# A hybrid retention and attention block: mean squares from a second, token-major load of x, a reordered opening, and re-dealt helper work

## The chip, the cores and the metric

The kernel runs on one core of a Trainium2 chip. The metric is the device time of one execution in microseconds (us); the median of three runs is compared. A core has five engines with instruction streams of their own: TensorE (matmuls), VectorE, ScalarE, GpSimd and SyncE. In the profile they are PE, DVE, ACT, POOL and SP. Each works through its stream in order and waits where an instruction needs something from another engine or from a DMA.

## The reference

One encoder layer over 1024 tokens with 16 learned meta tokens in front (T = 1040), D = 1024, all in float32. Cut to what matters:

```python
def _rms_norm(x, w):
    y = xf * lax.rsqrt(jnp.mean(xf * xf, axis=-1, keepdims=True) + EPS)
    return (y * w).astype(x.dtype)

u = RMSNorm(h)                 # h: meta tokens, then x
z = u @ w_in                   # one combined projection: q, k, v, gates of both branches
A: bidirectional retention     # 4 heads of 128 (v: 256), 8 chunks of 128 and the meta chunk,
                               # decays exp(rel * log_gamma), forward and backward scans,
                               # k * k_decay summed into states, group norm, SiLU gate, projection
B: windowed attention (+-128)  # 8 heads, 2 key groups, rotary, meta keys always seen, sink logit,
                               # SiLU gate, projection
out = x + RMSNorm((sigmoid(gA) * yA + sigmoid(gB) * yB) @ w_out)
```

The mean of squares of each token is thus needed by everything behind the first normalisation. The kernel projects x times the norm's weight, without the division, and brings the division in later, per token, as a factor.

## The kernel before

**Products.** A float32 product is made of three matmuls of rounded parts: high by high, low by high and high by low (`mm3`, L75 to L81). Each matrix is split for it: the high part is a rounding copy (ScalarE or GpSimd), the low part is the original less the high part (VectorE: `dve_lo`, L94, for weights, L335 for x). x comes feature-major: eight k-tiles `xr0` to `xr7` of 128 features by 1040 tokens. Their high and low parts are `xh`, `xl` (tiles named `big`).

**The opening** (L262 to L396, pool "setup"). For each k-tile, ScalarE makes the high part (L333) and VectorE the low part (L335), and `qk0_mm(k)` issues 18 matmuls: q and k of retention head 0, in six accumulator banks (`pq`, `pk`), each `mm3` over one piece of the tokens. ScalarE squares each `xr` tile (L354), and VectorE adds the eight squares up (`add_square`, L327). The sum is split (`sqh`, `sql`), and 18 small matmuls with a tile of ones (`sums_by_rows`, L376) bring the sums into a bank `pms`, one row per token. From it VectorE makes `ms` (mean squares plus EPS, L385, L386), `r2` and `kdr` (the factors of k in the states). The decays of the heads come out of `dec` by a logarithm's series (L210 to L239: `exponentials`, `decays`, `decay_series`, `decay_exponents`) in tiny VectorE instructions, and become tables (`decay_table`: its argument `dd` on VectorE, L247, its exponential `DT` on ScalarE, L249).

**Evacuation and the first values.** `evac_qk0(i)` takes one of the six q and k banks through the rotary formula: three VectorE multiplications (L190 to L192) and an addition on GpSimd. `projT` gives the values of one token block: block 0 is the meta tokens (`pv0_0`, matmuls L165 and L167, from `xm`, which `pack_meta` packs at L157), blocks 1, 2 and so on use `mm3`. The accumulators of the tag "pj" have three banks. So `pv0_1` waits for evacuation 0 to free one, `pv0_2` for another, `pv0_3` for `pv0_0`'s and `pv0_4` for `pv0_1`'s, which `vh_1` (ScalarE, L494) and `vl_1` (VectorE, L94) read.

**Loads.** SyncE issues the loads in the order of the text, and ScalarE's queue carries the first half of `xr0` and two small ones, `dect` and `idx` (L288, L289). `load_w` loads two raw halves of a weight unit and splits them.

**What sets the order.** The framework puts the instructions of each engine in an order by simulating their times, and an instruction under `issue_after` (or `follow`) comes behind the one named there. In attention, a chunk's work is written with `fill` ahead of and behind its scores: `fill(n)` takes n units of matmul work from a list of generators (query projections, gate products), after the table `FILL`. Helper works, such as loading, scaling and splitting for later parts, start at the yields which the table `BEGUN` names: `half_w` (half of a weight's split), `sum_fetch`, `sum_scale` and `sum_row` (x tiles `xs` for sums by rows), `load_k`, `pre_low` (low part of early gate weights).

Of the kernel before, what the change touches and what calls it, by code (L numbers as in the profile page):

```python
# [7 lines left out]
F32 = mybir.dt.float32  # L8
R = mybir.dt.float32r
# [18 lines left out]
FILL = (((5, 6),) * 1 + ((5, 5),) * 1 + ((4, 4),) * 1 + ((4, 3),) * 1 + ((4, 5),) * 2 + ((4, 7),) * 1 + ((4,  # L28
        5),) * 1 + ((6, 4),) * 1 + ((4, 4),) * 1 + ((4, 3),) * 1 + ((4, 4),) * 1 + ((4, 5),) * 2 + ((1, 4),)
        * 1 + ((6, 3),) * 1 + ((4, 5),) * 2 + ((4, 4),) * 1 + ((5, 4),) * 1 + ((3, 4),) * 1 + ((4, 3),) * 1 +  # L30
        ((4, 4),) * 4 + ((5, 4),) * 1 + ((3, 4),) * 1 + ((4, 4),) * 1)
# [12 lines left out]
def block_kernel(ctx: ExitStack, tc: tile.TileContext, xT, x, w_in, w_rb, w_ab, w_out, vecs, dec, sink,  # L44
# [156 lines left out]
    ones, onef = (ra.tile([P, 2], t, name=n) for n, t in (("ones", R), ("onef", F32)))  # L201
# [24 lines left out]
    def decay_series():  # L226
        v = nc.vector
        for j in (15, 13, 11, 9, 7, 5, 3):
            v.scalar_tensor_tensor(acc, acc, 1.0 / j, ss, op0=ALU.add, op1=ALU.mult)
        v.scalar_tensor_tensor(acc, acc, 1.0, s_, op0=ALU.add, op1=ALU.mult)  # L230
        v.scalar_tensor_tensor(lg, acc, -2.0, lg, op0=ALU.mult, op1=ALU.add)
# [35 lines left out]
    with tc.tile_pool(name="setup", bufs=1, reuse_waits="tile") as st:  # L267
# [19 lines left out]
        with tc.issue_after(nc.scalar.activation(warm, warm, AF.Exp).ins):  # L287
            nc.scalar.dma_start(dect, dec.partition_broadcast(P))  # L288
            nc.scalar.dma_start(idx, tab[:, MW + 3 * P:])  # L289
# [6 lines left out]
        nc.sync.dma_start(xr[2], xT[2])  # L296
        nc.sync.dma_start(xr[3], xT[3])
# [3 lines left out]
        nc.sync.dma_start(cr, rope[0])  # L301
        nc.sync.dma_start(sr, rope[1])
        nc.sync.dma_start(tabt[:, 0:3 * P], tab[:, MW:MW + 3 * P])
# [17 lines left out]
        nc.vector.memset(onef, 1.0)  # L321
        nc.vector.tensor_copy(ones, onef)
        nc.vector.memset(ms, 1.0)
        low, squares, sums = None, [], {}

        def add_square(k):
            sums[k] = nc.vector.tensor_tensor(squares[k], squares[k - 1], squares[k], ALU.add).ins  # L327

        for k in range(KT):
            t = xr[k]  # L330
            parts = [(0, 528), (528, T)] if k == 0 else [(0, T)]
            for a, b in parts:
                nc.scalar.activation(xh[k][:, a:b], t[:, a:b], AF.Copy, scale=vec[:, k:k + 1])  # L333
                with tc.issue_after(sums[k - 2] if k > 3 else exponents) if k > 2 else ExitStack():
                    low = nc.vector.scalar_tensor_tensor(xl[k][:, a:b], t[:, a:b], vec[:, k:k + 1],  # L335
                                                         xh[k][:, a:b].bitcast(F32), op0=ALU.mult, op1=ALU.subtract)
            if k == 2:
                with tc.issue_after(low.ins):
                    decays()
                    decay_series()  # L340
                    exponents = decay_exponents()
                decay_columns()
            if k == 0:
                with tc.issue_after(low.ins), tc.issue_after(raised[1]):
                    exponentials()
                    nc.gpsimd.tensor_tensor(e, ecst[:, 0:8], na, ALU.pow)
            if k == 1:
                third()
            if k == 3:
                with tc.issue_after(exponents):  # L350
                    fifth()
            qk0_mm(k)
            squares.append(st.tile([P, T], F32, tag="sq", bufs=4, name=f"sq{k}"))
            nc.scalar.activation(squares[k], t, AF.Square)  # L354
# [3 lines left out]
        with tc.issue_after(low.ins):  # L358
            pack_meta()
            wv0 = load_w(w_in, U_V, act=True)  # L360

        add_square(KT - 1)
        with tc.issue_after(sums[KT - 1]):
            rotated = evac_qk0(0)
        sq = squares[-1]
        sqh, sql = (st.tile([P, T], R, name=n) for n in ("sqh", "sql"))
        nc.scalar.copy(sqh, sq)
        with tc.issue_after(rotated):
            split = dve_lo(sql, sq, sqh)
        pms = p1("pms")  # L370

        def sums_by_rows(k):
            for c in (k, 8)[:1 + k // 7]:
                a, b = cols(c)
                for i, t in enumerate((sqh, sql)):
                    nc.tensor.matmul(pms[0:b - a, 2 * c:2 * c + 2], t[:, a:b], ones, start=i == 0, stop=i == 1)  # L376

        with tc.issue_after(split):
            rotated = evac_qk0(1)
        vmeta0 = ra.tile([P, 272], F32, tag="ak", bufs=2, name="vmeta0")[0:NM, 0:256]  # L380
        first = [projT(wv0, 0, "pv0_0", vmeta0), projT(wv0, 1, "pv0_1"), projT(wv0, 2, "pv0_2", None, sums_by_rows)]
    with tc.issue_after(rotated):
        turned = evac_qk0(4)
    with tc.issue_after(turned):
        nc.vector.tensor_scalar(ms[0:NM, 0:1], pms[0:NM, 0:1], 1.0 / D, EPS, op0=ALU.mult, op1=ALU.add)  # L385
        nc.vector.tensor_scalar(ms[:, 1:9], pms[:, 2:18].rearrange("p (c e) -> p c e", e=2)[:, :, 0], 1.0 / D, EPS,  # L386
                                op0=ALU.mult, op1=ALU.add)
# [58 lines left out]
    def gen_qk(h):  # L446
        w = load_w(w_in, U_QK + h)
# [419 lines left out]
    with tc.issue_after(normed):  # L867
        evac_qk0(2)
        decay_table((0,))
        evac_qk0(3, 5)  # L870
# [478 lines left out]
    def attention():  # L1349
# [144 lines left out]
        for k in range(len(chunks)):  # L1494
# [20 lines left out]
            if k in (4, 17, 24):  # L1515
# [3 lines left out]
    BEGUN = {0: [(fetch_aq, 3)], 1: [(sum_fetch, 0)], 4: [(half_w, 'q', 3, 0)], 5: [(half_w, 'q', 3, 0)],  # L1519
             6: [(sum_scale, 0)], 9: [(half_w, 'q', 3, 1)], 10: [(sum_row, 0)], 11: [(sum_fetch, 1)],  # L1520
             13: [(half_w, 'q', 3, 1)], 16: [(sum_scale, 1)], 18: [(sum_row, 1)], 20: [(sum_fetch, 2)],
             26: [(sum_scale, 2)], 28: [(sum_row, 2)], 29: [(sum_fetch, 3)], 33: [(load_k,)],
# [4 lines left out]
             66: [(sum_fetch, 7), (pre_parts, 7)], 67: [(pre_low, 7)], 72: [(sum_scale, 7)],  # L1527
# [67 lines left out]
def arrange(inputs):  # L1595
# [5 lines left out]
    def units(w, order):  # L1601
# [13 lines left out]
        "x": con(x),  # L1615
        "w_in": units(i["w_in"][0], order),
# [30 lines left out]
```

## Time and profile before

| | |
|---|---|
| median of three runs | 1068.65 us (1067.05 to 1073.63) |
| the profiled execution's own time | 1069.26 us |
| its span | 1067.5 us |
| TensorE busy | 1046.2 us, 98% |
| VectorE busy | 860.0 us, 81% |
| ScalarE busy | 481.7 us, 45% |
| GpSimd busy | 206.5 us, 19% |
| mean granted clock of TensorE | 0.997 |

The span runs from the first to the last instruction in the trace; the own time holds 1.8 us around it. A row of the timeline has the start, the busy time, the engine, the line, the operation, and output<-input with their shapes; in brackets stands the idle time of the engine ahead of it and what ended it. A row of the groups has the total and the mean duration of one (ns). A row of the windows has the length, then the busy time and instruction count of each engine, the granted clock, the share of the DMA engines' time and GB/s.

### The profile page before, as it was taken

The page shows a single profiled execution, that of the slowest core. Times are in us where ns is not written, and L with a number is a line of the kernel's source. Part 1 is how long each engine was busy: PE and PEld are TensorE (multiplying, and loading weights), DVE is VectorE, ACT ScalarE, POOL GpSimd, SP SyncE. Part 2 cuts the span into 40 slices and gives each one's busy share as a digit, 9 for nine tenths or more (in the row PEclk, how much of TensorE's full clock was granted, in tenths as well). Part 3 has the DMA queues.
Part 4 walks back from the last instruction along what each step waited for, and adds up shares of the span by engine and source line. Part 5 has one row for each costly group of instructions (what it writes and reads, how often), then busy time and mean ns, then how long its engine had stood idle before and what let it go on. Part 6 is the DMA issues. An engine that isn't in the chain of part 4 may idle for free.

```text
span 1067.5 us, 17154 instructions
## 1 busy us (share of the span) xinstructions
PE 1046.2 (98%) x5863; PEld 904.3 (85%) x5863; DVE 860.0 (81%) x1764; ACT 481.7 (45%) x1058; POOL 206.5 (19%) x270
## 2 busy tenths in 40 slices
PE   8999999999999999998999999999999999999997
PEld 7898999999998898877997888888888888787886
DVE  7897788777988549796769988999799799767765
ACT  7141351512510236565667545455456546333433
POOL 3234324224345213322220000000000000110032
PEclk9999999999999999999999999999999999999999
DMA  7121111203113428568668779899934746789464
GB/s 287 40 71 39 61 41 60 84 10 110 60 55 104 151 68 238 177 209 254 212 201 292 235 228 334 282 348 349 360 128 158 247 168 222 231 207 340 115 118 79
DMA packets 109447, 186.10 MB, mean 174 GB/s; under 512 B 10880, under 2 KB 50176, under 8 KB 108544
## 3 DMA queue, kind: packets, MB, share of 16 engines
q1 hardware_dynamic: 105472, 178.44, 50.1%
q0 software_dynamic: 3456, 6.29, 3.9%
q8 instruction: 46, 0.75, 0.3%
q14 instruction: 41, 0.34, 0.1%
q10 hardware_dynamic: 432, 0.28, 0.1%
HBM read 123.36 MB, written 62.40 MB: 174 GB/s over the span
## 4 chain that ended last, share of the span: by engine, by line
PE 89%; DVE 5%; DMA 3%; issue 1%; ACT 1%; POOL 0%; SPq 0%; DVEq 0%; POOLq 0%; ACTq 0%
PE bz L79 8%; PE bz L78 8%; PE bz L80 8%; PE pv L78 3%; PE pv L79 3%; PE pv L80 3%; PE ba L79 2%; PE br L79 2%; PE paq L79 2%; PE paq L78 2%; PE paq L80 2%; PE br L80 2%; PE br L78 2%; PE ba L78 2%; PE ba L80 2%; PE bo L78 2%
## 5 line engine op out<-in xcount | busy, mean ns | idle before, releaser
L1231 POOL DMA_DIRECT2D mx_d<-c1a x4 | 3.7, 919 | 394.2 <-DVE c1a L1222 394.2
L80 PE MATMUL bz<-T,lhz 128*128 128x512 f32 x192 | 75.8, 395 | 0.0
L79 PE MATMUL bz<-T,llz 128*128 128x512 f32 x192 | 75.7, 394 | 0.0
L78 PE MATMUL pv<-wh,big 128*128 128x256 f32 x256 | 73.9, 289 | 1.3 <-DVE m_qk L192 1.3
L78 PE MATMUL bz<-T,lhz 128*128 128x512 f32 x192 | 75.2, 394 | 0.0
L79 PE MATMUL pv<-wh,big 128*128 128x256 f32 x256 | 73.9, 289 | 0.0
L80 PE MATMUL pv<-wl,big 128*128 128x256 f32 x256 | 73.3, 286 | 0.0
L79 PE MATMUL bz<-big,llz 128*128 128x512 f32 x176 | 69.7, 396 | 0.0
L80 PE MATMUL bz<-big,lhz 128*128 128x512 f32 x176 | 69.3, 394 | 0.0
L78 PE MATMUL bz<-big,lhz 128*128 128x512 f32 x176 | 68.9, 395 | 0.0
L1398 POOL TENSOR_SCALAR p<-p,den 128x352 f32<-128x352 f32 (+2 forms) x60 | 36.8, 626 | 111.2 <-DVE den L1391 102.3
L1388 ACT ACTIVATE p<-raw,nm 128x353 f32<-128x353 f32 (+2 forms) x64 | 36.0, 565 | 39.8 <-DVE nm L1385 39.7
L78 PE MATMUL paq<-big,wh 128*128 128x512 f32 x128 | 51.8, 405 | 0.0
L595 ACT ACTIVATE ost<-to,rnw 128x128 f32<-128x128 f32 x64 | 19.9, 364 | 69.7 <-PE to L590 54.5
L79 PE MATMUL paq<-big,wl 128*128 128x512 f32 x128 | 50.9, 398 | 0.0
L78 PEld LDWEIGHTS pv<-wh,big 128*128 128x128 f32 x256 | 49.1, 192 | 1.7 <-DVE m_qk L192 1.6
L80 PE MATMUL paq<-big,wh 128*128 128x512 f32 x128 | 50.4, 394 | 0.0
L79 PEld LDWEIGHTS pv<-wh,big 128*128 128x128 f32 x256 | 49.1, 192 | 0.2
L80 PEld LDWEIGHTS pv<-wl,big 128*128 128x128 f32 x256 | 49.0, 191 | 0.0
L79 PEld LDWEIGHTS bz<-T,llz 128*128 128x128 f32 x192 | 36.2, 188 | 8.5
L80 PEld LDWEIGHTS bz<-T,lhz 128*128 128x128 f32 x192 | 36.2, 188 | 8.4
L78 PEld LDWEIGHTS bz<-T,lhz 128*128 128x128 f32 x192 | 36.2, 188 | 8.4
(623 smaller groups left out, 3565.5 us busy)
## 6 DMA issues: line engine op xcount, KB each, us to landing
wrz<-in_w_in_dram SPq DMA_DIRECT2D x32, 512.0 KB, 6.0
wr<-in_w_in_dram SPq DMA_DIRECT2D x27, 512.0 KB, 3.8
e<-e SPq DMA_DIRECT2D x40, 256.0 KB, 4.7
we<-in_w_in_dram SPq DMA_DIRECT2D x16, 512.0 KB, 4.3
tg<-tg_d SPq DMA_DIRECT2D x32, 256.0 KB, 5.2
T<-preT SPq DMA_DIRECT2D x6, 1024.0 KB, 6.8
oTr_d<-ost SPq DMA_DIRECT2D x16, 256.0 KB, 2.1
aq_d<-aq SPq DMA_DIRECT2D x16, 256.0 KB, 2.2
```

The costliest lines, as they stand in the source:

```text
L78: nc.tensor.matmul(o, ah, bh, start=first, stop=False, **kw)
L79: nc.tensor.matmul(o, al, bh, start=False, stop=False, **kw)
L80: latest[:] = [nc.tensor.matmul(o, ah, bl, start=False, stop=last, **kw).ins]
L595: nc.scalar.activation(ost[0][:, e_, w0:w0 + P], to[:, P * e_:P * e_ + P], AF.Copy, scale=rnw[:, 2 * h + e_:2 * h + e_ + 1])
L1231: nc.gpsimd.dma_start(d, to, accum_op=ALU.add)
L1388: last["exp"] = nc.scalar.activation(p[:, 0:1 + wid], raw[e_][:, 0:1 + wid], AF.Exp, scale=-1.0, bias=nm_[:, e_:e_ + 1], accum_out=den[:, ...
L1398: nc.gpsimd.tensor_scalar(pt[e_][:, 0:wid], pt[e_][:, 0:wid], den[:, e_:e_ + 1], 1.0, op0=ALU.mult, op1=ALU.mult)
```

## The change

Five things are done.

1. **Mean squares.** The squares of `xr`, their sums, `sqh`, `sql`, `ones` and the 18 small matmuls are gone. In their place x is loaded a second time, token-major: `meta` (a new argument, 16 by 1024) and eight tiles of 128 tokens by 1024 features (`xt0` to `xt8`), into the buffers of the `xr` tiles. ScalarE squares each with scale D^-0.5 and its accumulator writes the sum of a row into a column of `ms`. VectorE adds EPS to it.
2. **VectorE's order in the opening** is a chain (`then`): low part of each k-tile first, the weight split of part 2 to 4 behind tile 1, of part 4 to 8 behind tile 3, the decay series in two pieces behind tiles 4 and 5, then packing and the splits of `wv0`.
3. **Loads.** `dect` and `idx` go out on SyncE behind `xr2`. Behind the `xr` tiles come the two halves of `wv0`, then `cr`, `sr`, `tab`, `meta` and the eight `xt` (a chain, `send`); the weights of head 1 follow.
4. **Evacuations** go 0, 1, 4, 2, 3, then the decay table of head 0, then `ms`, `r2`, `kdr`, then 5. Before they went 0, 1, 4, `ms`, 2, table, 3, 5.
5. **Attention.** `FILL` differs at five chunks: (5, 6) to (5, 4) at 0, (4, 4) to (6, 4) at 2, (4, 4) to (5, 4) at 9, (4, 5) to (3, 5) at 12, (4, 4) to (4, 2) at 24; its sum goes from 244 to 242. In `BEGUN`, `half_w` of q, 3, 0 starts at yield 2 rather than 4, `sum_row` 0 at 8 rather than 10, `load_k` at 27 rather than 33, `pre_low` 7 at 66 rather than 67.

```diff
-        with tc.issue_after(nc.scalar.activation(warm, warm, AF.Exp).ins):
-            nc.scalar.dma_start(dect, dec.partition_broadcast(P))
-            nc.scalar.dma_start(idx, tab[:, MW + 3 * P:])
+        nc.scalar.activation(warm, warm, AF.Exp)
...
         nc.sync.dma_start(xr[2], xT[2])
+        nc.sync.dma_start(dect, dec.partition_broadcast(P))
+        nc.sync.dma_start(idx, tab[:, MW + 3 * P:])
         nc.sync.dma_start(xr[3], xT[3])
...
+        at = [None]
+
+        def then(f):
+            with follow(*[x for x in at if x is not None]):
+                r = f()
+            if r is not None:
+                at[:] = [r if hasattr(r, "name") else r.ins]
...
+            if k == 1:
+                then(third)
+            if k == 2:
+                then(exponentials)
+                nc.gpsimd.tensor_tensor(e, ecst[:, 0:8], na, ALU.pow)
+            if k == 3:
+                then(fifth)
+            if k == 4:
+                then(decays)
+                then(lambda: decay_series(0, 4))
+            if k == 5:
+                then(lambda: decay_series(4, 8))
+                then(decay_log)
+                then(decay_exponents)
                 decay_columns()
...
-            squares.append(st.tile([P, T], F32, tag="sq", bufs=4, name=f"sq{k}"))
-            nc.scalar.activation(squares[k], t, AF.Square)
-            if k > 1:
-                with tc.issue_after(exponents if k == 2 else low.ins):
-                    add_square(k - 1)
...
+        for i, t in enumerate(raw_v):
+            send(t, w_in[U_V, :, 4 * i:4 * i + 4, :])
+        send(cr, rope[0])
+        send(sr, rope[1])
+        send(tabt[:, 0:3 * P], tab[:, MW:MW + 3 * P])
+        then(pack_meta)
+        for t in raw_v:
+            then(split_v(t, "apart"))
+
+        def row_squares(cs):
+
+            for c in cs:
+                n = cols(c)[1] - cols(c)[0]
+                t = st.tile([P, T], F32, tag="xr", bufs=KT, name=f"xt{c}")[0:n, 0:D]
+                send(t, x[P * (c - 1):P * c] if c else meta)
+                with follow(*at):
+                    nc.scalar.activation(t, t, AF.Square, scale=D ** -0.5, accum_out=ms[0:n, c:c + 1])
+
+        row_squares(range(9))
+        rotated = evac_qk0(0)
...
+    for i in (4, 2, 3):
+        with tc.issue_after(rotated):
+            rotated = evac_qk0(i)
     with tc.issue_after(rotated):
-        turned = evac_qk0(4)
...
+        decay_table((0,))
+        nc.vector.tensor_scalar(ms, ms, EPS, None, op0=ALU.add)
```

The first place is VectorE in the opening, from the low part of k-tile 3 on (`big_1` are low parts, `w_1` is the low part of head 0's weights in k-tiles 4 to 7, `sq` the sums of squares). Before:

```order
L327 TENSOR_TENSOR sq_253<-sq_230,sq_253 128x1040
L335 SCALAR_TENSOR_TENSOR big_1_111<-xr_148,vec,big_0_109 128x1040
L94 TENSOR_TENSOR w_1_1_158<-wr_1_156,w_1_0_157 128x1024
L327 TENSOR_TENSOR sq_293<-sq_253,sq_293 128x1040
L335 SCALAR_TENSOR_TENSOR big_1_112<-xr_149,vec,big_0_110 128x1040
L327 TENSOR_TENSOR sq_317<-sq_293,sq_317 128x1040
L335 SCALAR_TENSOR_TENSOR big_1_112<-xr_150,vec,big_0_110 128x1040
```

And of the change, with the small rows being the decay series:

```order
L329 SCALAR_TENSOR_TENSOR big_1_111<-xr_146,vec,big_0_109 128x1040
L95 TENSOR_TENSOR w_1_1_156<-wr_1_154,w_1_0_155 128x1024
L329 SCALAR_TENSOR_TENSOR big_1_112<-xr_147,vec,big_0_110 128x1040
L220 TENSOR_SCALAR e_128<-e 128x8
L221 RECIPROCAL e_128<-e_128 128x8
L329 SCALAR_TENSOR_TENSOR big_1_112<-xr_148,vec,big_0_110 128x1040
L222 TENSOR_TENSOR s__129<-e,e_128 128x8
L223 TENSOR_TENSOR ss<-s__129 128x8
```

No sum stands between the low parts any more, and all of the series but two instructions stands behind the low part of k-tile 5; before it stood ahead of the first of these rows.

The second place is ScalarE at the end of the opening, from the last high parts to the first values (`wh` is `wv0`'s high part, `vh` the high part of the values). Before:

```order
L333 ACTIVATE big_0_110<-xr_152,vec 128x1040
L354 ACTIVATE sq_363<-xr_150 128x1040
L354 ACTIVATE sq_386<-xr_151 128x1040
L119 CAST wh_0_420<-wr_0_416 128x1024
L119 CAST wh_1_424<-wr_1_417 128x1024
L354 ACTIVATE sq_409<-xr_152 128x1040
L169 COPY vmeta_447<-pv_0_448 16x256
L367 CAST sqh<-sq_409 128x1040
L494 CAST vh_0_611<-vmeta_447 16x256
L494 CAST vh_1_625<-pv_1_467 128x256
```

And of the change, from the fourth square on:

```order
L377 ACTIVATE xt_411,ms<-xt_411 128x1024
L170 COPY vmeta_442<-pv_0_443 16x256
L377 ACTIVATE xt_414,ms<-xt_414 128x1024
L377 ACTIVATE xt_417,ms<-xt_417 128x1024
L377 ACTIVATE xt_420,ms<-xt_420 128x1024
L250 ACTIVATE DT<-dd_532 128x128
L377 ACTIVATE xt_423,ms<-xt_423 128x1024
L377 ACTIVATE xt_426,ms<-xt_426 128x1024
L497 CAST vh_0_587<-vmeta_442 16x256
L497 CAST vh_1_601<-pv_1_462 128x256
```

The squares have moved behind the high parts and the splits of `wv0`, and the table's exponential `DT`, which stood behind `vh_3`, now stands ahead of the last two squares and of `vh_1`.

The third place is SyncE's queue behind the last `xr` tile. Before:

```order
L300 DMA xr_152<-in_xT_dram 128x1040
L301 DMA cr<-in_rope_dram 128x1040
L302 DMA sr<-in_rope_dram 128x1040
L303 DMA tabt<-in_tab_dram 128x384
L396 DMA sinkc<-in_sink_dram 128x8
L110 DMA wr_0_416<-in_w_in_dram 128x1024
L110 DMA wr_1_417<-in_w_in_dram 128x1024
```

And of the change, without the last tiles:

```order
L301 DMA xr_150<-in_xT_dram 128x1040
L398 DMA sinkc<-in_sink_dram 128x8
L357 DMA wr_0_383<-in_w_in_dram 128x1024
L357 DMA wr_1_384<-in_w_in_dram 128x1024
L357 DMA cr<-in_rope_dram 128x1040
L357 DMA sr<-in_rope_dram 128x1040
L357 DMA tabt<-in_tab_dram 128x384
L357 DMA xt_402<-in_meta_dram 16x1024
L357 DMA xt_405<-in_x_dram 128x1024
```

The first value weights (`wr`) now stand ahead of `cr`, `sr` and `tabt`, and the `xt` tiles stand behind those, ahead of the weights of head 1.

More of the change, by code (lines that the diff above doesn't have):

```diff
@@ L329, in block_kernel, with low @@
+        def low(k, a, b):
+            return nc.vector.scalar_tensor_tensor(xl[k][:, a:b], xr[k][:, a:b], vec[:, k:k + 1],
+                                                  xh[k][:, a:b].bitcast(F32), op0=ALU.mult, op1=ALU.subtract)
         for k in range(KT):
             t = xr[k]
-            parts = [(0, 528), (528, T)] if k == 0 else [(0, T)]
-            for a, b in parts:
+            for a, b in [(0, 528), (528, T)] if k == 0 else [(0, T)]:
                 nc.scalar.activation(xh[k][:, a:b], t[:, a:b], AF.Copy, scale=vec[:, k:k + 1])
-                with tc.issue_after(sums[k - 2] if k > 3 else exponents) if k > 2 else ExitStack():
-                    low = nc.vector.scalar_tensor_tensor(xl[k][:, a:b], t[:, a:b], vec[:, k:k + 1],
-                                                         xh[k][:, a:b].bitcast(F32), op0=ALU.mult, op1=ALU.subtract)
+                then(lambda: low(k, a, b))
+            if k == 1:
+                then(third)
@@ L365, in block_kernel @@
-        sq = squares[-1]
-        sqh, sql = (st.tile([P, T], R, name=n) for n in ("sqh", "sql"))
-        nc.scalar.copy(sqh, sq)
-        with tc.issue_after(rotated):
[L369 to L376, printed above, removed]
@@ new lines, in block_kernel, with send @@
+        sent = []
+        def send(o, i):
+            with follow(*sent):
+                sent[:] = [nc.sync.dma_start(o, i).ins]
+        split_v, wv0 = halves_w(U_V)
+        raw_v = [keep.tile([P, 4, 256], F32, tag="wr", bufs=2, name=f"wr{U_V}_{s}") for s in range(2)]
+        for i, t in enumerate(raw_v):
[4 more added lines that the diff above has]
+        then(pack_meta)
```

72 lines of the change are left out of this document (20 added, 52 removed).

## The prediction

> **What bounds the kernel now.** I read the page's busy times first, then the windows, then the chain of waits, then the groups of the opening and the rows of TensorE in it.
>
> ```profile
> PE 1046.2 (98%) x5863; PEld 904.3 (85%) x5863; DVE 860.0 (81%) x1764; ACT 481.7 (45%) x1058; POOL 206.5 (19%) x270
> core 0: us, PE busy (x) PEld busy (x) DVE busy (x) ACT busy (x) POOL busy (x), PEclk, DMA share, GB/s
> 10.00:20.00 10.00, 8.50 (x52) 7.53 (x53) 9.01 (x23) 10.00 (x11) 4.82 (x3) 1.00 1.03 416
> 20.00:30.00 10.00, 9.60 (x62) 8.52 (x61) 9.96 (x12) 6.18 (x7) 2.68 (x1) 1.00 0.33 109
> 30.00:40.00 10.00, 7.78 (x50) 6.92 (x49) 9.88 (x18) 1.73 (x3) 0.89 (x2) 0.86 0.31 105
> 150.00:250.00 100.00, 100.00 (x719) 93.31 (x718) 77.83 (x189) 29.09 (x83) 35.99 (x49) 1.00 0.19 59
> 400.00:550.00 150.00, 144.20 (x848) 126.91 (x847) 118.30 (x284) 91.49 (x234) 41.52 (x59) 1.00 0.73 223
> ```
>
> TensorE is busy for 1046.2 of the span's 1067.5 us, so all that waits can give is 21 us, plus matmuls that go away or ran at a lower clock. The windows say where that lies: from 150 to 250 us TensorE never stops, from 400 to 550 it misses 150 - 144.20 = 5.8 us, and in the first 40 us it misses several, while VectorE stands at 9.96 and 9.88 of 10. The chain of waits has these links in that stretch:
>
> ```profile
> 22.64 1.23 DVE sq L327
> 32.90 1.15 DVE sq L327
> 36.20 0.46 DVE m_qk L192
> ```
>
> They are VectorE's sums of squares and the rope evacuation behind them. So the opening (0 to about 50 us) is bound by VectorE, and the rest by TensorE. A microsecond that TensorE gains before 50 us stays gained, since it has no slack behind it to lose it in.
>
> **The change, part by part.** The span is 1067.5 us, the profiled execution's own time 1069.26, which is 0.6 above the median 1068.65; I subtract gains from both alike.
>
> ```profile
> L354 ACT ACTIVATE sq<-xr 128x1040 f32<-128x1040 f32 x8 | 8.5, 1066 | 1.8 <-DVE sq L327 1.8
> L327 DVE TENSOR_TENSOR sq<-sq,sq 128x1040 f32<-128x1040 f32 x7 | 8.6, 1235 | 0.0
> L335 DVE SCALAR_TENSOR_TENSOR big<-xr,vec,big 128x1040 fp32r<-128x1040 f32 x7 | 9.1, 1296 | 1.0 <-ACT big L333 1.0
> L94 DVE TENSOR_TENSOR sql<-sq,sqh 128x1040 fp32r<-128x1040 f32 x1 | 1.6, 1573 | 0.0
> L190 DVE TENSOR_TENSOR m_qk<-pk,cr 128x256 f32<-128x256 f32 x3 | 1.2, 413 | 0.0
> L190 DVE TENSOR_TENSOR m_qk<-pq,cr 128x512 f32<-128x512 f32 x2 | 1.4, 682 | 0.0
> L376 PE MATMUL pms<-ones,sql 128*128 128x2 f32 x8 | 2.0, 250 | 0.0
> ```
>
> VectorE loses the seven sums, 8.6 us, and `sql`, 1.6: 10.2 us, all of it on the engine that binds. ScalarE trades eight squares of 1040 columns for eight of 1024 and one of 16 rows, so about the same 8.5 us, and loses `sqh` (one more pass of that size, 1.05). Each of its new squares also reads out an accumulator; the nearest row for that is 0.19 us, quoted below, so nine of them are 0 to 1.7 us more. TensorE loses the 18 small matmuls.
>
> *Early start.* Two small loads leave ScalarE's queue, where they went out right behind the first half of tile 0.
>
> ```profile
> 1.49 0.33 ACTq L288 DMA_DIRECT2D dect<-in_dec_dram  x1
> 6.71 0.72 ACT L333 ACTIVATE big<-xr,vec 128x512 fp32r<-128x512 f32 x1 [2.39 <-DMA xr<-in_xT_dram]
> 8.78 1.17 ACT L333 ACTIVATE big<-xr,vec 128x1040 fp32r<-128x1040 f32 x1 [0.38 <-DMA xr<-in_xT_dram]
> 10.09 0.47 PE L78 MATMUL pq<-big,w 128*128 128x512 f32 x1 [0.46 <-ACT big L333]
> ```
>
> ScalarE waits 2.39 us for the second half of tile 0 and 0.38 for tile 1, and also does a square of 1.06 between them; k-tile 1 on TensorE starts at 10.09, behind it. With the small loads behind tile 2 and the square gone, k-tile 1 can start up to 1.06 + 0.46 = 1.5 earlier. If the tiles come no sooner nothing is gained. No row shows how long the small packets held the tiles up, so the bounds are 0 and 1.5; I take 1.0, nearer the upper end, as the square's 1.06 goes in any case. Gain 1.0.
>
> *Stalls in the k-tiles.* The rows are where the k-tile blocks of `qk0_mm` begin on TensorE (18 matmuls each), with two stalls.
>
> ```profile
> 15.83 0.39 PE L78 MATMUL pq<-big,w 128*128 128x512 f32 x1
> 19.27 0.73 PE L80 MATMUL pq<-big,w 128*128 128x512 f32 x2 [1.41 <-DVE big L335]
> 20.32 0.63 PE L78 MATMUL pq<-big,w 128*128 128x512 f32 x2
> 23.83 0.39 PE L78 MATMUL pq<-big,w 128*128 128x512 f32 x1
> 26.65 0.39 PE L78 MATMUL pq<-big,w 128*128 128x512 f32 x1
> 29.47 0.39 PE L78 MATMUL pq<-big,w 128*128 128x512 f32 x1
> 32.30 0.28 PE L165 MATMUL pv<-wh,xm 128*48 128x256 f32 x1
> ```
>
> An undisturbed block takes 29.47 - 26.65 = 2.82 us. Block 3 takes 20.32 - 15.83 = 4.49 and block 4 takes 23.83 - 20.32 = 3.51, together 2.4 us over, for low parts that wait in VectorE's line behind the sums and the decay series. Afterwards only low parts of 1.30 us (9.1 / 7) and one weight split of 1.2 precede them: 6 x 1.30 + 1.2 is 9 us for what TensorE takes 6 x 2.82 = 17 us to use. The decay series is behind low parts 4 and 5 and costs some 3 us of tiny instructions; by my sum low part 6 ends near 22.8 and is wanted near 24.5. Gain 2.4, and if that cover of 1.7 us were gone by a longer series, 0.5 of it would be lost. The six q and k accumulators then end at 10.1 - 1.0 + 7 x 2.82 = 28.8 in place of 32.30; call it 28.4 to 28.8.
>
> *Meta values to token block 1.* TensorE's next rows:
>
> ```profile
> 34.30 0.29 PE L165 MATMUL pv<-wh,xm 128*48 128x256 f32 x1 [0.90 <-DVE xm L157]
> 36.70 0.38 PE L78 MATMUL pv<-wh,big 128*128 128x256 f32 x1 [1.32 <-DVE m_qk L192]
> 45.85 0.36 PE L78 MATMUL pv<-wh,big 128*128 128x256 f32 x1
> 48.86 0.28 PE L78 MATMUL pv<-wh,big 128*128 128x256 f32 x1
> 37.50:38.00 0.50, 0.50 (x4) 0.50 (x4) 0.50 (x1) 0.00 (x0) 0.00 (x0) 0.50 0.00 0
> 40.00:40.50 0.50, 0.50 (x4) 0.50 (x4) 0.50 (x1) 0.00 (x0) 0.50 (x1) 0.50 0.00 0
> ```
>
> A k-tile block streams 24 x 256 columns in 2.82 us, so 256 columns take 0.1175. `pv0_0` is 16 such passes, 1.9 us; it took 36.70 - 32.30 = 4.40, of which 0.90 is a wait for the last packing of meta tokens and 1.32 one for evacuation 0, which frees `pv0_1`'s bank. Both follow the sums in VectorE's line. Without these the packing is done by about 27 and evacuation 0 ends about 1.4 us (0.43 + two half-height ones of the 0.41 kind) after its accumulator is complete, near 28.7, while `pv0_0` runs till about 30.3. Gain 4.40 - 1.88 = 2.5.
>
> *Token blocks 1 and 2.* `pv0_1` and `pv0_2` are 48 passes, 5.64 us; they took 45.85 - 36.70 = 9.15. The surplus of 3.5 is two things. The granted clock is 0.50 in the rows at 37.5 and 40.0, and 3.4 us at half clock lose about 1.6 us; the other 1.9 us are the 18 small matmuls (16 of them in blocks, 8 at 250 ns being 2.0 of busy time with overlap). The matmuls go in any case, the lower clock goes if the idle time ahead of it goes. Gain 3.5, or 1.9 if the clock drops all the same.
>
> The clock drop came after 0.90 + 1.32 us of waits within 2.4 us. The Trainium skill, "TensorE: Matmul & The Clock Gate", section "What's actually happening", has the clock halve only after an idle window of about 3.4 us. By it neither those waits nor the wait below would lower the clock; the rows at 37.5 and 40.0 speak against it here, and only the length of the lower clock, 3.4 us, agrees with its window. By the rule the next term would cost no clock, and rival B below would be 1061.2.
>
> *The new wait.* What is late next is the line in ScalarE. `pv0_4` needs `pv0_1`'s bank, freed by `vh_1` on ScalarE and `vl_1` on VectorE, and `vh_1` now stands behind all nine squares, with the decay table's exponential between the seventh and the eighth. That exponential waits for VectorE, which does evacuations 0, 1, 4, 2 and 3 first: 27.4 + 1.3 x 4 + 2.0 (the 512-wide one at 0.68 + two smaller) + 0.4 for the meta values, and 0.9 for the table's argument, so near 36. Then come the exponential, 0.4, two squares of 1.05, and `vh_0` and `vh_1`: to 39.3 or, with an accumulator readout of 0.19 each, 39.7. `vl_1` is done by 40.5, behind the mean squares on VectorE (they used to wait for the small matmuls):
>
> ```profile
> 46.02 0.14 DVE L385 TENSOR_SCALAR ms<-pms 16x1 f32<-16x1 f32 x1 [4.10 <-PE pms L376]
> 424.00 0.19 ACT L1388 ACTIVATION_READ_ACCUMULATOR p<-raw,nm 128x1 f32 x1
> ```
>
> TensorE would be there at 30.3 + 5.64 + 3 us for two transposes and `pv0_3` = 39.05. So it waits 1.4 us. The bounds are 0 (an evacuation less deep in the line) and 3.0 (1.4 with a new drop of the clock, 1.6). I take 1.4, nearest to the chain above. Behind `vh_1` on ScalarE stand `vh_2` and `vh_3`, whose banks have a block's time more; after that VectorE is ahead, since evacuations 2 and 3 and the table are already done.
>
> The token-major load is 4.26 MB. At 416 GB/s (the row from 10 us) it takes 10.2 us. Starting where before's loads thin out, near 22 us, it lands near 32; at the mixed rate of the attention, 223 / 0.73 = 305 GB/s, 14 us and 36. The last square is due at about 37.6. It is hidden, with 1.6 to 5 us of cover.
>
> *Opening:* 1.0 + 2.4 + 2.5 + 3.5 - 1.4 = 8.0 us.
>
> *Attention.* Eight units of filling work move between chunks and two leave the table (units not spent in it run right after the last chunk); four helper works begin earlier. No matmul is added or taken away. Two of its larger waits:
>
> ```profile
> 480.51 0.50 PE L79 MATMUL pe<-big,wel 128*128 128x512 f32 x1 [1.44 <-DVE wel L94]
> 491.97 0.55 PE L1409 MATMUL pt<-ident,p 128*128 128x128 f32 x3 [1.43 <-POOL p L1398]
> 486.43 0.72 ACT L750 ACTIVATE xs<-xs,vec 128x512 f32<-128x512 f32 x1 [4.70 <-DMA xs<-in_xT_dram]
> ```
>
> At 486.43 ScalarE stood 4.70 us for a half of `xs`, and five microseconds on TensorE waited 1.43. In the changed program that second half is loaded right behind the first, which helps, but both scalings now stand ahead of the exponentials of that chunk, which would hold them if the load is late. The bounds are 5.8 gained (all waits) and 4 lost (that stall reaching TensorE in full, less its present 1.43, or a like one elsewhere). I take 0.5 gained, the middle, since the matmul order hardly differs.
>
> **Sum:** 8.0 + 0.5 = 8.5. Profiled 1069.26 becomes 1060.8, the median 1068.65 becomes 1060.2.
>
> **The rivals.** *A, the attention mends more:* the waits at 480 and 491 go, and the small ones near them do not, 3 us more: 1057.2. For it, half_w and the sum of rows begin two yields sooner and the second `xs` load comes earlier; against it, the wait for `wel` has another cause (a VectorE line) that the rows moved don't touch.
> *B, the start comes no sooner and the new wait drops the clock:* 1.0 + 1.6 back, 1062.8. For it, 2.2 us of waits sufficed before; against it, one wait of 1.4 is less.
> *C, slower:* the token-major load is late. It shares the queue with all that comes before, and the row-wise tiles wait for buffers of the feature-major ones. Each microsecond by which the last tile lands after 37.6 moves `vh_1`, and so TensorE, by one. The gain is eaten up when it lands at 46, a rate of 4.26 / 24 = 178 GB/s, and 1% is lost at 57; a landing at 57 would give 1080. For it, 109 GB/s in the row from 20 us; against it, that row has a DMA share of only 0.33.
> *D, it does not do what it says:* VectorE's freed time is handed back, because the squares on ScalarE hold what the sums held before (each evacuated bank and `vh` behind an in-order line), so that only the small matmuls and the early start go: 1068.65 - 1.9 = 1066.8. Against it, the squares have no reader on TensorE before `vh_1`.
>
> **How the numbers follow.** Forecast 0.47, with a range of its own from 1057.5 to 1063; A 0.27, B 0.14, C 0.06, D 0.06. The range is 1055.5 (A with the early start at its 1.5 and a smaller wait) to 1066.5 (B with 4 us lost in the attention); C and most of D stay out. A measurement of this kernel tells about 1% from no change, that is 1058.0 and 1079.3. A lies two thirds below 1058.0, 0.18, the forecast a sixth, 0.08: faster 0.26. Slower by over 1% is C at its worst and an unseen stall, 0.05. The rest, 0.69, is within.
>
> **What would show it.** Right: blocks 1 to 7 on TensorE 2.82 us apart; no wait ahead of `pv0_1`; the granted clock 1.00 from 30 to 40; a wait of about 1.4 ahead of `pv0_4` with VectorE's `vl` as its releaser; and mean squares on VectorE behind the last square near 38.7. Wrong: the first matmul of k-tile 1 still at 10.1 (early start), a wait in block 6 or 7 (the series), the last square ended by a load rather than by the exponential (C), or more than 6 us idle from 390 to 540 (attention).

## The result, and the profile after

The changed kernel takes 1065.77 us (median of 20 runs, 1063.12 to 1068.95), the kernel before 1068.44 (20 runs, 1066.68 to 1073.63). The ratio is 0.9975, with an interval from 0.9965 to 0.9984: 2.7 us faster, where 8.5 were forecast. The profiled execution of the changed kernel took 1067.77 us, 2.0 above its median, and its span is 1066.0, 1.5 below the span before.

The first lines are the page's busy times and the windows of the first 50 us of the changed kernel.

```profile
PE 1046.8 (98%) x5845; PEld 904.6 (85%) x5845; DVE 849.2 (80%) x1753; ACT 484.6 (45%) x1067; POOL 212.4 (20%) x270
core 0: us, PE busy (x) PEld busy (x) DVE busy (x) ACT busy (x) POOL busy (x), PEclk, DMA share, GB/s
10.00:20.00 10.00, 10.00 (x64) 9.09 (x64) 8.97 (x22) 8.40 (x8) 3.40 (x2) 1.00 1.03 406
20.00:30.00 10.00, 10.00 (x65) 9.05 (x64) 6.55 (x19) 5.31 (x9) 5.79 (x1) 1.00 1.03 386
30.00:40.00 10.00, 10.00 (x87) 9.82 (x87) 8.65 (x18) 5.42 (x11) 4.30 (x5) 1.00 0.67 270
40.00:50.00 10.00, 8.40 (x65) 7.67 (x65) 7.50 (x20) 3.70 (x12) 4.32 (x4) 1.00 0.00 0
```

TensorE is busy without a break from 10 to 40 us, where it had 8.50, 9.60 and 7.78 of 10 before, and VectorE is no longer full. The token-major load moves 386 and 270 GB/s and is over by 37 us. So the opening did change in the way described. But TensorE's busy total rose from 1046.2 to 1046.8 although 18 matmuls are gone, which says that some of it ran slower. These rows of TensorE, ScalarE and VectorE in the changed kernel's timeline say where time is still lost:

```profile
6.98 0.80 PE L79 MATMUL pq<-big,w 128*128 128x512 f32 x1 [0.85 <-ACT big L335]
7.78 1.16 ACT L335 ACTIVATE big<-xr,vec 128x1040 fp32r<-128x1040 f32 x1 [0.86 <-DMA xr<-in_xT_dram]
8.00 0.63 PE L80 MATMUL pq<-big,w 128*128 128x512 f32 x1
11.01 0.39 PE L79 MATMUL pq<-big,w 128*128 128x512 f32 x1
30.77 0.28 PE L166 MATMUL pv<-wh,xm 128*48 128x256 f32 x1
39.01 0.31 ACT L250 ACTIVATE DT<-dd 128x128 f32<-128x128 f32 x1 [2.68 <-DVE dd L249]
40.27 1.04 ACT L377 ACTIVATE xt<-xt 128x1024 f32<-128x1024 f32 x1
41.43 0.17 DVE L390 TENSOR_SCALAR ms<-ms 128x9 f32<-128x9 f32 x1 [2.46 <-ACT xt L377]
43.35 0.39 PE L79 MATMUL pv<-wh,big 128*128 128x256 f32 x1 [1.60 <-DVE vl L95]
120.63 0.33 PE L500 MATMUL tr<-ident,kr 128*128 128x128 f32 x1 [0.61 <-ACT ost L598]
```

K-tile 1 starts at 11.01 (10.09 before), since the 512-column matmuls of k-tile 0 still take 0.63 us at 8.00; at full clock they take 0.39. From there the seven blocks run to 30.77 at 19.76 / 7 = 2.82 each. The fifth token block waits 1.60 us, behind the exponential `DT` (itself 2.68 us behind VectorE) and the last two squares. It starts at 43.35, against 48.86 before. A wait of 0.61 in the retention is new.

The lead of the changed kernel over the one before at some places of the program, read off the two traces as a difference of start times:

| place | changed kernel, profiled execution |
|---|---|
| k-tile 1 | 0.9 later |
| first matmul of `pv0_0` | 1.5 earlier |
| fifth token block | 5.5 earlier |
| first values of attention (361.58 before, 358.83 after) | 2.8 earlier |
| end of the span | 1.5 earlier |

So the lead of 5.5 us at the end of the opening, itself below the forecast 8.0, is mostly given back behind it. Of the 2.75 us lost between that block and the first values of attention, 0.75 are waits near 120 us (TensorE is busy for 129.25 of the 130 us from 60 to 190, for all 130.00 before). Some 1.7 more are a window of 3.41 us at half clock right behind them, shown below. The opening-alone kernel, whose trace has no half clock there, gives back 1.5.

### The profile page after: what moved, and what is told of

Same layout as the page of the kernel before. It is cut to its first block, busy times and chain, and to the rows that moved or that the text cites. A ratio compares the mean times of both kernels' runs of the same rounds, so it can differ in the third digit from the quotient of the medians.

```text
span 1066.0 us, 17137 instructions
## 1 busy us (share of the span) xinstructions
PE 1046.8 (98%) x5845; PEld 904.6 (85%) x5845; DVE 849.2 (80%) x1753; ACT 484.6 (45%) x1067; POOL 212.4 (20%) x270
## 4 chain that ended last, share of the span: by engine, by line
PE 94%; DVE 2%; DMA 1%; ACT 1%; issue 0%; SPq 0%; DVEq 0%; POOLq 0%; ACTq 0%
PE bz L80 8%; PE bz L81 8%; PE bz L79 8%; PE paq L80 3%; PE paq L79 3%; PE paq L81 3%; PE pv L79 3%; PE pv L81 3%; PE pv L80 3%; PE ba L80 2%; PE br L80 2%; PE br L79 2%; PE br L81 2%; PE ba L81 2%; PE ba L79 2%; PE bo L79 2%
## 5 line engine op out<-in xcount | busy, mean ns | idle before, releaser
L1399 POOL TENSOR_SCALAR p<-p,den 128x352 f32<-128x352 f32 (+2 forms) x60 | 39.7, 674 | 107.7 <-DVE den L1392 82.8
```

Of the source, the lines that this page charges most:

```text
L1399: nc.gpsimd.tensor_scalar(pt[e_][:, 0:wid], pt[e_][:, 0:wid], den[:, e_:e_ + 1], 1.0, op0=ALU.mult, op1=ALU.mult)
```

## The experiments

**The opening and the tables apart.** The first kernel takes the change without its attention tables, the second the tables without the rest.

```diff
# e1_opening_only: the changed kernel with the tables of before
-FILL = (((5, 4),) * 1 + ((5, 5),) * 1 + ((6, 4),) * 1 + ...
+FILL = (((5, 6),) * 1 + ((5, 5),) * 1 + ((4, 4),) * 1 + ...
# e2_tables_only: the kernel before with the changed FILL and BEGUN
```

> The changed kernel with the attention's two tables (FILL, BEGUN) of before: the opening alone. Theory S (the forecast gain of the opening came in part only: 5.5 us at the fifth token block, and was given back behind it by new stalls and by windows at half clock): the tables matter little, so this comes out near the changed kernel, 1065.0 to 1066.5 us, 2 to 3 below before. Theory T (the opening kept its gain and the new tables cost it): 1060 to 1063.

> The kernel before with the changed FILL and BEGUN alone. Theory S: idle time of TensorE from 390 to 550 us falls by about 0.5, the time is 1067.5 to 1068.5. Theory T: 3 us or more slower than before, 1071 or above.

Measured: the opening alone 1066.62 us (12 runs), ratio 0.9980 to before, interval 0.9968 to 0.9993. The tables alone 1067.94 (12 runs), ratio 0.9993, interval 0.9982 to 1.0005. Windows over the attention, of before, of the tables alone and of the opening alone:

```profile
390.00:550.00 160.00, 154.20 (x901) 135.52 (x900) 126.18 (x303) 98.30 (x250) 45.19 (x64) 1.00 0.70 213
...
390.00:550.00 160.00, 155.24 (x909) 136.41 (x908) 125.66 (x305) 98.94 (x252) 50.63 (x66) 1.00 0.71 213
...
390.00:550.00 160.00, 155.20 (x905) 136.67 (x904) 125.02 (x303) 98.60 (x250) 45.64 (x64) 0.99 0.71 216
```

TensorE misses 5.8, 4.8 and 4.8 us there. The last kernel has the old tables and yet as little idle time as the second, so executions differ by as much as the tables do. Theory T falls: the tables didn't cost the gain. What is lost is lost with the opening alone.

**The new wait.** The table of head 0 is made behind `kdr`, so that its exponential no longer stands ahead of the last squares.

```diff
     with tc.issue_after(rotated):
-        decay_table((0,))
         nc.vector.tensor_scalar(ms, ms, EPS, None, op0=ALU.add)
...
+    with tc.issue_after(normed):
+        decay_table((0,))
```

> The changed kernel with the decay table of head 0 moved behind the factors kdr, so that its exponential no longer stands ahead of the last two squares on ScalarE. If the wait of 1.6 us ahead of the fifth token block comes from that chain (squares, vh, vl), it goes: the block starts within 0.2 us of the end of the fourth and the time falls by 1.0 to 1.6 to 1064.2 to 1064.8. If the line on VectorE is late by itself, a wait of 1 us or more stays and the time is 1065 to 1066.5.

Measured: 1063.70 us (6 runs, 1063.37 to 1064.59), ratio 0.9954, interval 0.9935 to 0.9972. Rows of this kernel's timeline and its window from 30 to 60 us, and the same window of the changed kernel:

```profile
36.36 1.06 ACT L377 ACTIVATE xt<-xt 128x1024 f32<-128x1024 f32 x1
37.54 0.42 DVE L389 TENSOR_SCALAR ms<-ms 128x9 f32<-128x9 f32 x1 [1.02 <-ACT xt L377]
30.00:60.00 30.00, 30.00 (x252) 29.34 (x250) 25.31 (x66) 15.94 (x42) 12.54 (x15) 1.00 0.23 91
...
30.00:60.00 30.00, 28.40 (x235) 27.50 (x235) 24.47 (x63) 15.04 (x40) 10.90 (x14) 1.00 0.23 91
```

The last square now starts at 36.36 rather than 40.27, and the wait of 1.60 is gone: 30.00 busy of 30, as in the three other profiles with this edit. The wait's cause is shown. Its price is not: this set's median is 2.1 us below the changed kernel's, more than the wait itself, and a second set (below) is 0.2 below.

**The start.** K-tile 0's matmuls of the first half of the tokens are put ahead, since TensorE waited 0.85 us for the second half while they were ready.

```diff
-            for m0, a, b, o in outs:
-                mm3(...)
+            for m0, a, b, o in outs if k else sorted(outs, key=lambda t: t[2] > 528):
+                with tc.issue_after(latest[0]) if k == 0 and latest else ExitStack():
+                    mm3(...)
```

> The changed kernel with k-tile 0's matmuls of the first half of the tokens written ahead of those of the second, so that TensorE has work while the second half is loaded. Theory C (a gap of 0.85 us in the first blocks lets the half clock last one window of 3.4 us longer, to 10.46 in the trace): full clock by 8.5 us in every execution, k-tile 1 starts near 9.2 in place of 11.0, and the median falls by 1 to 2, to 1064 or 1065. Rival (the order of k-tile 0 is covered by the wait for tile 1's high part near 8.95): k-tile 1 starts at 9 to 10 whatever the clock, and the median is within 0.5 of the changed kernel's 1065.8.

Measured: 1064.72 us (12 runs), ratio 0.9961, interval 0.9945 to 0.9976, so 1.0 below the changed kernel, with intervals that overlap. In the profiled execution k-tile 1 starts at 9.59, later than 9.2, having waited 0.38 for its high part. The opening alone, with the unchanged order, had an execution in which the clock came early:

```profile
7.60 0.40 PE L80 MATMUL pq<-big,w 128*128 128x512 f32 x1
9.66 0.47 PE L78 MATMUL pq<-big,w 128*128 128x512 f32 x1 [0.25 <-ACT big L334]
```

There the matmuls take 0.40 at 7.60, and k-tile 1 starts at 9.66. So 0.4 us is the most that the early start is worth at full clock (10.09 - 9.66). When the clock comes late the start is 0.9 later than before. That the new order makes the clock come early isn't shown: its two profiled executions have full clock from 5.6 and 5.0 us, but four others with the order of the changed kernel (`c2_after_again`, `e1_opening_only`, `e3_late_table`, `e9_late_table_again`) have it from 4.6 to 6.6 us as well.

**Both edits.** The next kernel has both.

> The changed kernel with both edits: the decay table behind kdr, and k-tile 0's matmuls of the first half ahead. If the two gains are apart (2.1 and 1.0 us below the changed kernel), 1062.5 to 1063; if they are one, 1063.5 to 1064.

Measured: 1064.96 us (12 runs, 1063.03 to 1068.04), ratio 0.9971. The gains did not add up. Its runs have a mean granted clock of 0.9953, against 0.9967 for each edit alone, which is 1.5 us of 1065 (the mean clock of one kernel differs between sets of runs too, as the second set of the late table below shows). Its profiled execution had three windows of half clock, from 121.1, 264.4 and 489.7 us.

**Other executions of the two kernels.** Nothing is edited here.

> The kernel before, unchanged, to see the half-clock windows of another execution. Theory C (the clock follows windows of 3.413 us that run free of the program, so the same waits fall into one window or into two): in another execution the first full clock comes at another time than 6.39 us, and a window of half clock behind an attention wait of 1.4 us can appear or the one near 37 us go. The mean granted clock differs between executions by 0.001 to 0.003 and the time goes with it, about 1 us per 0.001. If the drops belong to fixed places of the program, all executions have the same clock within 0.001.

> The changed kernel, unchanged. Theory C: the late full clock (10.46 us) and the drops at 123 and 492 us are not all there again; the idle times are: 1.6 us ahead of the fifth token block, 0.6 near 120.6, 1.5 near 490. Rival: the drops stand at the same places again.

Measured: before 1068.48 us (11 runs), changed 1065.72 (11 runs), ratio 0.9975, interval 0.9966 to 0.9985. In all the traces the changes of the granted clock lie a whole number of times 3.413 us apart, and each spell of half clock in mid-program lasts 3.413. The rows below are cut at those places. First before, then before in the other execution:

```profile
33.69:37.11 3.42, 1.49 (x11) 1.17 (x12) 3.36 (x8) 1.32 (x2) 0.39 (x1) 1.00 0.69 247
37.11:40.52 3.41, 3.41 (x18) 3.41 (x18) 3.35 (x5) 0.40 (x1) 1.03 (x2) 0.50 0.00 0
...
32.31:35.72 3.41, 2.13 (x17) 1.43 (x15) 3.40 (x6) 0.33 (x2) 0.00 (x0) 1.00 0.78 249
35.72:39.13 3.41, 2.49 (x21) 2.49 (x22) 3.35 (x6) 1.40 (x3) 0.77 (x1) 1.00 0.15 59
39.13:42.55 3.42, 3.42 (x33) 3.40 (x32) 2.67 (x5) 0.38 (x1) 1.34 (x2) 1.00 0.02 5
```

It is the same program with the same two waits (0.90 and 1.32 before, 0.91 and 1.29 here). Where they fall into one window, leaving 1.49 us of work, the next window runs at 0.50. Where a boundary parts them, 2.13 and 2.49 are left and no clock is lost. The windows run free of the program, and where they lie is a matter of chance. Then the changed kernel, first execution:

```profile
3.63:7.05 3.42, 2.57 (x8) 1.77 (x7) 1.20 (x3) 1.37 (x2) 0.81 (x2) 1.00 0.94 277
41.18:44.59 3.41, 1.81 (x15) 1.61 (x15) 3.08 (x11) 2.05 (x8) 1.81 (x1) 1.00 0.00 0
44.59:48.01 3.42, 3.42 (x28) 3.16 (x27) 3.38 (x7) 0.00 (x0) 1.90 (x2) 1.00 0.00 0
119.69:123.10 3.41, 2.66 (x17) 1.78 (x15) 3.18 (x11) 1.73 (x6) 0.69 (x3) 1.00 0.21 77
123.10:126.51 3.41, 3.41 (x17) 3.17 (x16) 2.70 (x9) 1.60 (x6) 0.71 (x2) 0.50 0.02 5
488.33:491.74 3.41, 1.33 (x8) 0.79 (x7) 3.41 (x9) 2.32 (x6) 1.91 (x1) 1.00 0.81 243
491.74:495.15 3.41, 3.08 (x8) 2.60 (x9) 1.36 (x4) 1.45 (x4) 1.09 (x2) 0.50 0.97 228
```

(In the first row the clock column is not to be trusted: the trace's clock records begin at 10.46, and the durations above show the half clock till then.) That window has 0.85 us of waiting and did not bring the full clock. The new wait of 1.60 lies in the window from 41.18 and does not lower the clock behind it. The small wait near 120.6 does, though TensorE is busy for 2.66 of 3.41 there: that window is full of transposes and of matmuls on 16 rows. The attention wait of 1.51 near 490 does too. In the second execution of the changed kernel the drop near 122 is there again, the one near 492 isn't:

```profile
118.68:122.09 3.41, 2.66 (x16) 1.79 (x14) 3.18 (x12) 1.87 (x7) 0.82 (x2) 1.00 0.22 77
122.09:125.51 3.42, 3.42 (x17) 3.27 (x16) 2.55 (x9) 1.41 (x6) 0.57 (x2) 0.50 0.02 5
```

So theory C holds for the drops near 37 and 490, and its rival in part for the one near 122. Over the profiled executions of all kernels, the drop near 37 us is in 3 of 4 with the old opening; the one near 122 in 5 of the 8 with the new opening and an unedited retention, in none of 4 with the old; one in the attention, at 475 to 500 us, in 7 of 9 with the new opening and in 1 of 4 with the old. The mean granted clock over many runs tells the sum: 0.9965 before (35 runs), 0.9960 for the changed kernel (20 runs). The clock did not get better. The 0.5 us by which it looks worse are no more than sets of runs of one kernel differ by: the sets of before lie between 0.9961 (15 runs) and 0.9968 (11 runs). That each execution's time goes with its clock by 1 us per 0.001 was expected too strongly: runs of before at 0.997 spread from 1064.22 to 1069.76, so clock isn't all that differs.

**The small loads.** `dect` and `idx` go back to ScalarE's queue.

```diff
-        nc.scalar.activation(warm, warm, AF.Exp)
+        with tc.issue_after(nc.scalar.activation(warm, warm, AF.Exp).ins):
+            nc.scalar.dma_start(dect, dec.partition_broadcast(P))
+            nc.scalar.dma_start(idx, tab[:, MW + 3 * P:])
...
-        nc.sync.dma_start(dect, dec.partition_broadcast(P))
-        nc.sync.dma_start(idx, tab[:, MW + 3 * P:])
```

> The changed kernel with the loads of dect and idx back on ScalarE's queue, where they were. The forecast's early start (1.0 us from these loads and the square that left): k-tile 1's high part would start at 8.8 as before or later, against 7.8 to 8.4. If the loads don't matter, it starts between 7.8 and 8.5 and the time is that of the changed kernel within 0.7 us. The matmuls of k-tile 0 happen to come in another order (the first half's low by high ahead), which by theory C brings the full clock sooner, 0.5 to 1 us.

Measured: 1064.95 us (11 runs), ratio 0.9971, interval 0.9958 to 0.9983. K-tile 1's high part starts at 8.67, near the 8.8 of before, and its matmuls at 9.98. That is 0.3 later than the 9.66 above, but executions with the loads in their new place start k-tile 1 anywhere from 9.66 to 10.04 at full clock, so no price of the loads' place is shown, by the trace or by the median.

**The price of the small matmuls.** Each of the 18 is done twice in the kernel before.

```diff
-                for i, t in enumerate((sqh, sql)):
+                for _ in range(2):
+                    for i, t in enumerate((sqh, sql)):
...
```

> The kernel before with each of the 18 small matmuls of the sums done twice. The forecast put 1.9 us on them. If that is their price, the stretch from the first matmul of token block 2 to the first transpose grows by 1.9 us; if the surplus of 3.5 us was mostly the half clock, by 0.5 to 1.0 us.

The first small matmul and the first transpose behind them, of this kernel and of before in the undisturbed execution:

```profile
41.16 0.17 PE L377 MATMUL pms<-ones,sqh 128*16 128x2 f32 x1
49.91 0.27 PE L498 MATMUL tr<-ident,kr 128*16 128x128 f32 x1
...
39.91 0.17 PE L376 MATMUL pms<-ones,sqh 128*16 128x2 f32 x1
46.91 0.27 PE L497 MATMUL tr<-ident,kr 128*16 128x128 f32 x1
```

8.75 us against 7.00: 1.75 for eighteen more. The forecast's 1.9 holds. The time of this kernel, 1073.57 us, is a single run with a mean clock of 0.995, so it prices nothing.

**The wait in the retention.** These are the first transposes of the next head's keys, first in before, then in the changed kernel:

```profile
124.63 0.27 PE L497 MATMUL tr<-ident,kr 128*16 128x128 f32 x1
124.66 0.37 PE L79 MATMUL pv<-wh,big 128*128 128x256 f32 x1
125.69 0.27 PE L497 MATMUL tr<-ident,kr 128*128 128x128 f32 x1
...
119.75 0.27 PE L500 MATMUL tr<-ident,kr 128*16 128x128 f32 x1
120.63 0.33 PE L500 MATMUL tr<-ident,kr 128*128 128x128 f32 x1 [0.61 <-ACT ost L598]
```

Before, matmuls of values fill the time between the two transposes; in the changed kernel nothing does. On top of the late table, the third chunk's transposes go behind the next head's second chunk.

```diff
-            if c < NB - 1:
+            if 1 < c < NB - 1:
                 finish(c + 2)
         state["n", 1]()
-        pend.extend([lambda: finish(2), lambda: finish(1)])
+        pend.extend([lambda: finish(3), lambda: finish(2), lambda: finish(1)])
```

> The changed kernel with the late decay table, and in the retention the transposes of the third chunk's output (finish(3) at the end of a head's backward loop) put off behind the next head's second chunk, like those of chunks 1 and 2. If the wait of 0.6 us near 120 us and the half-clock window that follows it in many executions come from the transposes' bank, both go: idle time from 60 to 190 us falls from 1.1 to 0.5 or less, the mean granted clock rises, and the time is 0.5 to 1.5 below that of the late table alone (1063.7). Otherwise it is within 0.5 of it or above.

> The changed kernel with the late decay table once more, beside the above: 1063.3 to 1064.5 if the first result holds.

Measured: 1065.41 us (9 runs) with it, ratio 0.9970, interval 0.9957 to 0.9983; 1065.58 (7 runs, 1062.08 to 1066.62) for the late table alone, ratio 0.9958, interval 0.9941 to 0.9974. The windows, first of the edited kernel, then of the late table alone (its first profile), and behind them a row of the edited kernel's timeline:

```profile
60.00:190.00 130.00, 129.13 (x964) 121.88 (x964) 103.28 (x253) 39.66 (x119) 47.54 (x65) 1.00 0.18 58
190.00:390.00 200.00, 198.07 (x1372) 181.94 (x1371) 148.58 (x360) 58.40 (x164) 64.58 (x85) 1.00 0.26 82
...
60.00:190.00 130.00, 128.86 (x961) 121.41 (x960) 103.59 (x258) 40.21 (x122) 49.30 (x66) 1.00 0.18 59
190.00:390.00 200.00, 198.74 (x1376) 182.80 (x1376) 147.17 (x357) 58.17 (x163) 65.76 (x84) 1.00 0.26 82
...
120.68 0.38 PE L79 MATMUL pkv<-vh,khf 128*128 128x256 f32 x1 [0.34 <-ACT khf L511]
```

The wait of 0.61 is gone, and one of 0.34 stands a little behind its place. So idle time falls by only 0.27 in the first stretch, to 0.87 where 0.5 was expected, and grows by 0.67 in the second. The drop near 122 isn't in its trace and its mean clock is 0.9974 rather than 0.9953, the higher of the two, yet the time isn't better. It is no improvement, and whether removing the wait removes the drop stays open, as one execution without it proves little. The late table held its ratio (0.9954 and 0.9958 in two sets), the lowest of these kernels, but its second median missed the expected 1063.3 to 1064.5. The medians put it 4.5 and 3.7 us below the kernel before. The interval of every edited kernel overlaps that of the changed kernel, so no edit's gain over it is shown by the time alone.

## Why the prediction was right or wrong

The direction was right and the size was not: 8.5 us were forecast and 2.7 measured. 1065.77 lies inside the range, but near its upper end, which stood there for rivals that did not happen.

- **Stalls in the k-tiles (2.4), right.** Seven blocks at 2.82 in the changed kernel.
- **Meta values to token block 1 (2.5), right.** `pv0_0` takes 1.9 us and no wait stands ahead of `pv0_1`.
- **The 18 small matmuls (1.9 of the 3.5), right:** 1.75 by doubling them.
- **The new wait (1.4), right in place, cause and size:** 1.60, and moving the table removes it. (A slip in its sum: 30.3 + 5.64 + 3 is 38.94, not 39.05, which would have made it 1.6.)
- **The token-major load is hidden (rival C), right:** it is over by 37 us, while the last square starts at 40.27 behind `DT`. With the late table the last tile lands at 36.28 and its square starts at 36.36, so the load is then next in line. Nor is rival D what happened: TensorE did gain 5.5 us up to the fifth token block.
- **Attention (0.5), right within what executions differ by.** Rival A's 3 us more did not come.
- **The early start (1.0), mis-sized.** The forecast counted the square's 1.06 as gone "in any case". But its own row had ScalarE waiting 0.38 for the load of tile 1 behind that square, and the load still sets the start: with no square there, ScalarE waits 0.86 for it. At full clock k-tile 1 starts at 9.66, 9.76, 9.81 and 10.04 in four executions with the changed order, and at 9.71, 9.98, 10.02 and 10.09 in the four of the old opening, so 0.4 is the most that it gave. Where the clock was at half it starts at 11.01 (here) and 11.20 (`e8_finish_later`), about 1 later than before. That wasn't in the bounds of 0 to 1.5.
- **The lower clock (1.6 of the 3.5), the step that failed.** The forecast took a spell at half clock from one trace, put it down to the waits ahead of it, and booked it as a cost that goes with them. But it is in only 3 of 4 executions of the old opening. It does go, as none of the nine of the new opening has it near 37 us, and others came: near 122 us and more often in the attention. A gain of 1.6 us would be a rise of the mean clock by 0.0015; it went from 0.9965 to 0.9960. So the 1.6 are all missing of the 5.8 us by which the gain fell short, and perhaps 0.5 more.
- **"A microsecond that TensorE gains before 50 us stays gained", wrong.** The new wait near 120.6 takes 0.75 us with a smaller one beside it, or more, in every profile of the new opening with the retention unedited. The window at half clock behind it, in 5 of those 8, takes 1.7 more (part of the clock's term above). And the end of the program is 0.43 longer behind the last matmul in all of them (7.42 us idle from 1000 us on, 6.98 before; the cause wasn't sought). The wait comes with the order that the scheduler gave the next head's first products, as the rows above show; why it chose that order stays open. The doubled small matmuls, on the old opening, had 0.76 us of idle time in that stretch too (0.00 in the other three profiles of the old one), so a shift of the opening can deal it without this change. The forecast followed the order of the opening and the attention, not of the retention in between.

Together 1.6 (clock) + 0.6 (early start) + 0.75 + 0.43 + 0.2 (the new wait) are 3.6 of the missing 5.8, and 4.1 with the uncertain 0.5 of the clock. The other 1.7 to 2.2 can't be assigned: two executions of the kernel before differ by 2.4 us in what is left when the half clock is taken off (idle time and work at full clock, 1063.3 and 1065.7), so a pair of profiles doesn't tell it.

The row and the rule on the clock gate stood against each other in the forecast. The Trainium skill, "TensorE: Matmul & The Clock Gate", section "What's actually happening", gives a free-running window of 3413 ns. The trace agrees: the changes of the clock here lie a whole number of 3.413 us apart. Its condition, an idle window of that length, is not what the traces show: windows in which TensorE was busy for 1.33, 1.49 and 2.66 of 3.41 us were followed by half clock, while one with 1.81 of 128-row matmuls was not. By the rule none of these drops would have come; the measurements decide against that part.

## What to carry to other kernels

A spell of half clock in one profile is a draw, not a price: cut the trace at the clock's own boundaries, look at a second execution and at the mean clock of all runs before counting it as gained or lost. When an engine that bound a stage is relieved, look up which in-order line is late next (here the exponential ahead of the squares); that part of the forecast held to 0.2 us. And a gain at the front of a scheduled program has to be followed through the stages behind it, since the scheduler deals their order anew.

## What the runs showed of the hardware

The granted clock of TensorE changes only at boundaries 3.413 us apart, whose place against the program's start differs from execution to execution (first full clock from 4.3 to 10.5 us). Whether a window lowers the clock doesn't go by busy time alone: 2.66 us of transposes and of 16-row matmuls lowered it, 1.81 us of full matmuls didn't. That the kind of matmul is what counts is argued from these windows; no run varied it alone. A squaring pass with an accumulator over 128 by 1024 took 1.04 to 1.06 us and its readout 0.18, most of it beside the next pass (three of them from 33.11 to 36.33).
